# Up-projection, first pair of column blocks: the seventh product is subtracted earlier, and the spread of 1/rms stands one product later

## The chip, the cores and the metric

The kernel runs on one core of a Trainium2 chip. The core has a matrix engine (TensorE, PE in the profile, with PEld for its weight loads), a vector engine (VectorE, DVE), an engine for activations and copies (ScalarE, ACT), a further elementwise engine (GpSimd, POOL) and queues that issue DMA transfers (SyncE, SP, is the one used most). Each engine works through its own list of instructions in order, and waits for the others through semaphores. The metric is the time of one execution on the device, in microseconds (us); smaller is better.

## The reference

The program computes one layer of a decoder: normalisation, two attention branches with gates, a projection back, a residual sum, and then a gated feed-forward part with a short convolution, and a last normalisation. The change lies in the feed-forward part, whose heart is this:

```python
def rmsnorm(x, w):
    xf = x.astype(jnp.float32)
    y = xf * lax.rsqrt(jnp.mean(xf * xf, axis=-1, keepdims=True) + EPS)
    return (y * w.astype(jnp.float32)).astype(x.dtype)
...
def conv_ffn(xn, w_up, conv_w, conv_b, w_down):
    S = xn.shape[1]
    u = xn @ w_up
    upad = jnp.pad(u, ((0, 0), (CONV_WIDTH - 1, 0), (0, 0)))
    c = conv_b
    for j in range(CONV_WIDTH):
        c = c + upad[:, j:j + S] * conv_w[j]
    gate, val = jnp.split(c, 2, axis=-1)
    return (jax.nn.silu(gate) * val) @ w_down
...
        xn = rmsnorm(x, norm_ffn_w[l])
        x = x + conv_ffn(xn, w_up[l], conv_w[l], conv_b[l], w_down[l])
```

The sequence has 1024 positions, the model 1024 channels, and the up-projection 2 x 2816 columns. Everything is float32.

## The kernel before

All activations are kept transposed, channels on the 128 partitions and the 1024 positions along the free axis. A float32 product is made of three matmuls on parts: each operand is split into a high part (`wh`, `sh`, `B_..h`) and a low part (`wl`, `sl`, `B_..l`), and high by high, high by low and low by high are added up in PSUM, the accumulators that PE writes, which has eight banks. ACT makes the high part by a cast, DVE the low part by a subtraction; a *split* below is such a pair (lines 122 and 123).

The up-projection is the function `hidden`. Its 44 blocks of 128 columns are done in 22 pairs: block j of the gate half goes with block j + 22 of the value half. A pair is computed by a scheme of Strassen's kind, with seven products of half size in place of eight: P1, P2, P5, P7, P3, P6 and P4. Each is 12 matmuls of 128x512 (`product`, lines 877 to 885) into one bank. POOL makes the sums and differences of the weight blocks that the scheme needs (`sf`, lines 98 to 104), and these are then split (`sh`, `sl`). Afterwards the function `recombine` adds the products up into the four quarters of the result, `us`: a copy of P1 by ACT into `s1` (L426), and seven operations of DVE (L427 P2, L428 P6, L429 P7 into `u3`, L430 and L431 P5, L432 P3, L433 P4). A product's bank can be written again when the last of these has read it.

The normalisation is put off until after the product: the weights `norm_ffn_w` are multiplied into the operands, and the factor 1/rms of each position, `rstd`, is multiplied onto `us` when it is read for the convolution (L1038; on DVE for the first pair, on POOL for the others). 1/rms comes out of a sum over channels as a column of numbers per block of positions (`rs`, L197). To have it along the free axis on every partition, PE transposes it, broadcast, against the identity: this is the *spread* (`spread`, L203), in two halves of four transposes each, into the two banks of the pool `psC`. ACT copies each half into `rstd` (L966). For the first pair, one of these two banks held the sums over channels, `ssq`, and the other holds the product P4, since the six banks of the pool `psF` hold the other products. So the spread's second half can only be written when L433 has read P4.

Then the convolution follows in halves (`glu_halves`): two multiplications by `rstd`, an ACTIVATE of ACT with the centre tap and the bias (L1044), two operations of DVE with the other taps (L1046), Silu (L1048), the product with the value half (L1049) and a store to memory (`hd`, L1050).

The order of the instructions on each engine is set by a scheduling layer between this code and the program. It goes by its own estimate of when operands are ready, and by priorities; `issue_after(x)` makes what is issued within it stand behind instruction x on its engine. So a change at one place can move rows of other engines for some distance.

The first pair's order of work on PE is: the first three quarters of P1, P2, P5, P7, P3, then their last quarter and the sums over channels, then P6 and P4, then the first two products of the second pair (P1, P2), which need no waiting, then the spread, then the rest of the second pair.

Of the kernel before, what the change touches and what calls it, by code (L numbers as in the profile page):

```python
# [13 lines left out]
ALU = mybir.AluOpType  # L14
# [8 lines left out]
H2 = 512  # L23
# [20 lines left out]
class Trunk:  # L44
# [372 lines left out]
                        self.keep(m, u, (tp, "hi"))  # L417
        self.uw = self.w22 = None

    def recombine(self, ps, us, tp, o):  # L420

        nc = self.nc
        c11, c12, c21, c22 = (us[w][:, o + hf * H2:o + (hf + 1) * H2] for w in range(2) for hf in range(2))
        s1, u3 = (self.tl(tp, [P, H2], n, bufs=1) for n in ("s1", "u3"))
        tt = nc.vector.tensor_tensor
        nc.scalar.copy(s1, ps["P1"])  # L426
        tt(c11, ps["P2"], s1, ALU.add)  # L427
        tt(s1, ps["P6"], s1, ALU.add)  # L428
        tt(u3, ps["P7"], s1, ALU.add)  # L429
        tt(c22, ps["P5"], u3, ALU.add)  # L430
        tt(s1, ps["P5"], s1, ALU.add)  # L431
        tt(c12, ps["P3"], s1, ALU.add)  # L432
        return tt(c21, u3, ps["P4"], ALU.subtract)  # L433

    def keep(self, m, u, to):

# [432 lines left out]
    def product(self, ps, a, b, ks=range(4), first=True, last=True, skip=False, low_last=False):  # L869

        nc = self.nc
        ks = list(ks)
        ah, al = a
        if low_last:
            for n, k in enumerate(ks):
                for i, x in enumerate(self.B[b, k]):
                    nc.tensor.matmul(ps, ah[:, k, :], x, start=first and n == i == 0, stop=False, skip_group_check=skip)  # L877
            for n, k in enumerate(ks):
                nc.tensor.matmul(ps, al[:, k, :], self.B[b, k][0], start=False, stop=last and n == len(ks) - 1, skip_group_check=skip)
            return  # L880
        for n, k in enumerate(ks):
            bh, bl = self.B[b, k]
            nc.tensor.matmul(ps, ah[:, k, :], bh, start=first and n == 0, stop=False, skip_group_check=skip)  # L883
            nc.tensor.matmul(ps, ah[:, k, :], bl, start=False, stop=False, skip_group_check=skip)  # L884
            nc.tensor.matmul(ps, al[:, k, :], bh, start=False, stop=last and n == len(ks) - 1, skip_group_check=skip)  # L885

    def hidden(self, pair):
        nc, tc = self.nc, self.tc
        with ExitStack() as ctx:
# [6 lines left out]
            prods = (("P1", "A11", "B11"), ("P2", "A12", "B21"), ("P5", "S1", "T1"), ("P7", "S3", "T3"),  # L896
                     ("P3", "S4", "B22"), ("P6", "S2", "T2"), ("P4", "A22", "T4"))
# [3 lines left out]
            for j in range(NF):  # L901
                w, ps = ready.pop(j) if j else (w0, {})
                if j == 0:
# [10 lines left out]
                    tp = e(tc.tile_pool(name="tp", bufs=2, side="right", reuse_waits="tile"))  # L914
# [3 lines left out]
                    for n, (name, a, b) in enumerate(prods[:5]):  # L918
                        self.product(ps[name], w[a], b, (3,), first=False)
                        if n == 4:  # L920
                            self.col_sums(ssq, [self.rstd], NB, 0)
                            with tc.high_priority(400):
                                rs = self.rstd_cols(ssq, 8, D)
# [12 lines left out]
                us = [self.tl(tp, [P, T + 2], "us", bufs=3) for _ in range(2)]  # L936
                if j == NF - 1:
# [5 lines left out]
                    self.deep = True  # L943
                    with tc.high_priority(100):
                        self.ahead(2)
                c21 = self.recombine(ps, us, tp, 2)
                made = []
                if j < NF - 1:

                    self.after = c21 if j else None  # L950
                    w, ps = ready[j + 1] = self.next_w(), {}
                    self.after = None
                    if j:
                        made = [x[y] for x, y in ((w, ("made", "A22")), (self.wq[-1], ("made", "A11"))) if y in x]
                    if j == NF - 2:
                        raw = [self.tl(self.sfp[0], [P, T], "t42", bufs=1)] + [self.tl(self.sfp[0], [P, T], "sf") for _ in range(2)]
                        for k, r in enumerate(raw):
                            nc.sync.dma_start(r, self.hd[k])
                    for name, a, b in prods[:2 if j == 0 else 0]:
                        ps[name] = self.tl(psF, [P, H2], "t")  # L960
                        self.product(ps[name], w[a], b, low_last=name == "P1")
                if j == 0:
                    for hf in range(2):
                        sp = self.tl(self.psC, [P, H2], "c")
                        self.spread(sp, rs, hf * 4)
                        nc.scalar.copy(self.rstd[:, hf * H2:(hf + 1) * H2], sp)  # L966

                if j < NF - 2:
                    with ExitStack() as queue:
                        for i in made:  # L970
                            for x in i:
                                queue.enter_context(tc.issue_after(x.ins))
                        self.glu_halves(j, us)
                    continue
# [326 lines left out]
```

## Time and profile before

| what | value |
|---|---|
| time, median of 3 runs | 1354.51 us (1354.1 to 1355.41) |
| profiled execution, its time | 1354.84 us |
| profiled execution, its span from first to last instruction | 1353.1 us |
| mean granted clock of TensorE | 0.996 |
| up-projection in that span | about 690 to 1110 us |

In the profile's rows, an engine's name is followed by the source line, the operation, and the tiles that it writes and reads, output first. In a timeline the first two numbers are the start and the length in us; a bracket at the end gives the idle time of the engine just ahead of the row and what ended it. "xN" is the number of instructions in a row. In a list of waits, the three numbers are the sum in us, the number of waits and the longest. The names in these rows leave out the buffer numbers: `t` is a bank of the pool `psF`, `c` one of `psC` (or, from L1044 on, a buffer of the convolution), `s` is `s1` and `u` is `u3`.

### The profile page before, as it was taken

The numbers are of one execution on the slowest core, as the hardware profiler recorded it, in microseconds if no ns is written. First come the engines' busy times: TensorE is split into PE (matmuls) and PEld (weight loads), VectorE is DVE, ScalarE is ACT, GpSimd is POOL, SyncE is SP. The second block draws the span as 40 slices with busy tenths as digits, with TensorE's granted clock in tenths as the row PEclk, the third lists the DMA queues.
The fourth block names the chain that finished last, engine by engine and source line by source line (L and its number), as shares of the span: only waits on it lengthen the run. The fifth ranks groups of instructions, "written<-read, shape, count | busy, mean of one in ns | idle before, by whom it ended". The sixth has DMA issues, their size and how long they took to land.

```text
span 1353.1 us, 17298 instructions
## 1 busy us (share of the span) xinstructions
PE 1330.8 (98%) x6304; PEld 1105.7 (82%) x6304; DVE 1036.0 (77%) x1557; ACT 619.0 (46%) x1003; POOL 467.2 (35%) x349
## 2 busy tenths in 40 slices
PE   7999999999999999999998999999999999999997
PEld 6888888888887877878887888888888888888887
DVE  7846775288899875365679999999999977986454
ACT  8432232276667664334445344443444434333343
POOL 0436652010102125641454655555554510231011
PEclk9999999999999999999999999999999999999998
DMA  6423443966554236234422222222122238552342
GB/s 256 154 106 152 139 151 140 262 172 177 156 133 140 76 116 225 106 124 140 158 94 91 94 74 83 94 78 92 68 91 76 84 129 314 198 178 72 94 139 79
DMA packets 62468, 179.48 MB, mean 133 GB/s; under 512 B 6832, under 2 KB 15152, under 8 KB 62384
## 3 DMA queue, kind: packets, MB, share of 16 engines
q1 hardware_dynamic: 50928, 160.98, 36.5%
q10 hardware_dynamic: 11456, 17.41, 3.5%
q8 instruction: 49, 0.80, 0.2%
q14 instruction: 35, 0.29, 0.1%
HBM read 129.61 MB, written 48.76 MB: 132 GB/s over the span
## 4 chain that ended last, share of the span: by engine, by line
PE 87%; POOL 4%; DMA 3%; DVE 3%; issue 1%; ACT 1%; POOLq 0%; SPq 0%; ACTq 0%; DVEq 0%
PE t L883 13%; PE t L884 13%; PE t L885 13%; PE y L1086 3%; PE d L1086 3%; PE t L877 3%; PE sc L599 3%; PE g L180 3%; PE g L181 3%; PE g L182 3%; PE y L1113 2%; PE d L1113 2%; DMA gr<-gd 2%; PE sc L182 2%; PE sc L181 2%; PE sc L180 2%
## 5 line engine op out<-in xcount | busy, mean ns | idle before, releaser
L122 ACT CAST sh<-sf 128x1024 fp32r<-128x1024 f32 x62 | 65.1, 1051 | 111.4 <-PE t L884 91.8
L1046 DVE SCALAR_TENSOR_TENSOR c<-us,vecs,c 128x512 f32<-128x512 f32 x160 | 110.1, 748 | 4.3 <-ACT c L1044 4.3
L145 ACT CAST wh<-raw 128x1024 fp32r<-128x1024 f32 (+2 forms) x60 | 60.9, 1014 | 105.6 <-PE sc L181 30.5
L1038 POOL TENSOR_TENSOR us<-us,rstd 128x1024 f32<-128x1024 f32 x38 | 98.1, 2598 | 12.6 <-DVE us L433 5.3
L123 DVE TENSOR_TENSOR sl<-sf,sh 128x1024 fp32r<-128x1024 f32 x62 | 92.8, 1499 | 12.0 <-ACT sh L122 11.8
L147 DVE TENSOR_TENSOR wl<-raw,wh 128x1024 fp32r<-128x1024 f32 (+2 forms) x60 | 75.2, 1256 | 32.0 <-ACT wh L145 20.6
L1044 ACT ACTIVATE c<-us,vecs 128x512 f32<-128x512 f32 x80 | 61.2, 781 | 62.6 <-POOL us L1038 60.4
L123 DVE TENSOR_TENSOR wl<-raw,wh 128x1024 fp32r<-128x1024 f32 (+1 forms) x35 | 76.0, 2170 | 3.7 <-ACT wh L122 3.6
L98 POOL TENSOR_TENSOR sf<-rv 128x512 f32<-128x512 f32 x30 | 41.3, 1376 | 100.5 <-DVE sl L123 57.8
L180 PE MATMUL g<-xh,wh 128*128 128x512 f32 x176 | 70.7, 402 | 0.1
L182 PE MATMUL g<-xh,wl 128*128 128x512 f32 x176 | 70.4, 400 | 0.0
L181 PE MATMUL g<-xl,wh 128*128 128x512 f32 x176 | 70.3, 399 | 0.0
L197 POOL TENSOR_TENSOR rs<-ms,mhalf 128x8 f32<-128x8 f32 (+2 forms) x9 | 14.5, 1607 | 157.2 <-DVE ms L195 146.6
L103 POOL TENSOR_TENSOR sf<-raw,rv 128x512 f32<-128x512 f32 x30 | 40.7, 1357 | 67.3 <-DVE sl L123 67.3
L603 DVE CUSTOM_DVE_ANT_0 L<-sc,bias 128x128 f32<-128x128 f32 (+7 forms) x64 | 47.8, 752 | 17.0 <-PE sc L599 13.9
L604 ACT ACTIVATE L<-L,sm 128x128 f32<-128x128 f32 (+7 forms) x64 | 49.6, 779 | 20.0 <-DVE sm L603 17.3
L582 POOL MEMSET aT<- 128x128 f32 x32 | 6.2, 205 | 151.6 <-PE t L628 97.9
L757 POOL TENSOR_TENSOR gr<-gr,rstd 128x1024 f32<-128x1024 f32 x16 | 40.1, 2509 | 43.1 <-DMA gr<-gd 43.0
L1048 ACT ACTIVATE c<-c 128x512 f32<-128x512 f32 x40 | 24.0, 600 | 59.4 <-DVE c L1046 59.4
L599 PE MATMUL sc<-u,u 128*128 128x512 f32 (+2 forms) x192 | 49.7, 358 | 0.0
L182 PE MATMUL sc<-mh,wl 128*128 128x512 f32 x126 | 49.1, 390 | 0.2 <-DVE wl L147 0.2
L180 PE MATMUL sc<-mh,wh 128*128 128x512 f32 x126 | 49.0, 389 | 0.0
(515 smaller groups left out, 4330.8 us busy)
## 6 DMA issues: line engine op xcount, KB each, us to landing
u<-qd SPq DMA_DIRECT2D x72, 256.0 KB, 6.4
raw<-in_w_down SPq DMA_DIRECT2D x27, 512.0 KB, 3.7
raw<-in_w_in SPq DMA_DIRECT2D x25, 512.0 KB, 4.2
hr<-hd SPq DMA_DIRECT2D x50, 256.0 KB, 5.5
raw<-in_w_up SPq DMA_DIRECT2D x23, 512.0 KB, 3.4
hd<-c SPq DMA_DIRECT2D x22, 512.0 KB, 2.6
rv<-in_w_up SPq DMA_DIRECT2D x21, 512.0 KB, 3.4
gr<-gd SPq DMA_DIRECT2D x16, 512.0 KB, 3.5
```

The costliest lines, as they stand in the source:

```text
L123: j = nc.vector.tensor_tensor(lo, src, hi.bitcast(F32), ALU.subtract)
L147: self.lo = (eng or nc.vector).tensor_tensor(wl, raw, wh.bitcast(F32), ALU.subtract)
L180: nc.tensor.matmul(ps, wh[:, kc + o, :], ah, start=first and n == 0, stop=False)
L181: nc.tensor.matmul(ps, wh[:, kc + o, :], al, start=False, stop=False)
L182: nc.tensor.matmul(ps, wl[:, kc + o, :], ah, start=False, stop=last and n == len(kcs) - 1)
L599: nc.tensor.matmul(sc[:, lo + n0:lo + n1], qs, k[c][part][:, n0:n1], start=part == 0, stop=part == 1)
L883: nc.tensor.matmul(ps, ah[:, k, :], bh, start=first and n == 0, stop=False, skip_group_check=skip)
L884: nc.tensor.matmul(ps, ah[:, k, :], bl, start=False, stop=False, skip_group_check=skip)
L885: nc.tensor.matmul(ps, al[:, k, :], bh, start=False, stop=last and n == len(ks) - 1, skip_group_check=skip)
L1038: (nc.vector if j == 0 else nc.gpsimd).tensor_tensor(u[:, 2:], u[:, 2:], self.rstd, ALU.mult)
L1046: nc.vector.scalar_tensor_tensor(c, u[:, o + k:o + k + H2], col(m, k), c, ALU.mult, ALU.add)
L1086: nc.tensor.matmul(ps, v[:, n, :], x, start=n == i == 0, stop=n == len(js) - 1 and i == 2)
```

## The change

Three things are changed, all at the border between the first and the second pair:

1. `recombine` has a switch, `p4`, set for the first pair: the subtraction of P4 is written right behind `u3`, ahead of the two operations on P5. It gives no result then; the one that it gave was not used for the first pair.
2. The loop for the products that run ahead of the spread takes three in place of two, so the second pair's P5 is done ahead of the spread. The second half of the spread is ordered behind the last matmul of that product.
3. For the second pair, the copy of P1 into `s1` is ordered on ACT behind the spread's second copy.

`product` now gives back its last matmul, so that it can be used in the ordering.

```diff
-    def recombine(self, ps, us, tp, o):
+    def recombine(self, ps, us, tp, o, p4=False, after=None):
...
-        nc.scalar.copy(s1, ps["P1"])
+        with self.tc.issue_after(after.ins) if after is not None else nullcontext():
+            nc.scalar.copy(s1, ps["P1"])
         tt(c11, ps["P2"], s1, ALU.add)
         tt(s1, ps["P6"], s1, ALU.add)
         tt(u3, ps["P7"], s1, ALU.add)
+        if p4:
+            tt(c21, u3, ps["P4"], ALU.subtract)
         tt(c22, ps["P5"], u3, ALU.add)
         tt(s1, ps["P5"], s1, ALU.add)
         tt(c12, ps["P3"], s1, ALU.add)
-        return tt(c21, u3, ps["P4"], ALU.subtract)
+        return None if p4 else tt(c21, u3, ps["P4"], ALU.subtract)
...
-                c21 = self.recombine(ps, us, tp, 2)
+                c21 = self.recombine(ps, us, tp, 2, j == 0, made if j == 1 else None)
...
-                    self.after = c21 if j else None
+                    self.after = c21
...
-                    for name, a, b in prods[:2 if j == 0 else 0]:
+                    for name, a, b in prods[:3 if j == 0 else 0]:
                         ps[name] = self.tl(psF, [P, H2], "t")
-                        self.product(ps[name], w[a], b, low_last=name == "P1")
+                        last = self.product(ps[name], w[a], b, low_last=name == "P1")
                 if j == 0:
                     for hf in range(2):
                         sp = self.tl(self.psC, [P, H2], "c")
-                        self.spread(sp, rs, hf * 4)
-                        nc.scalar.copy(self.rstd[:, hf * H2:(hf + 1) * H2], sp)
+                        with tc.issue_after(last.ins) if hf else nullcontext():
+                            self.spread(sp, rs, hf * 4)
+                        made = nc.scalar.copy(self.rstd[:, hf * H2:(hf + 1) * H2], sp)
...
-                        for i in made:
+                        for i in made if j else ():
```

In the new file the lines of `recombine` behind its copy are one to three lines further down (L432 is P4 of the first pair, L433 and L434 P5, L435 P3, L436 P4 of the others), the copy into `rstd` is L971, the multiplication L1043 and the matmuls of `product` L886 to L888. The rows below show where the instructions stand, buffer numbers included.

On PE, at the end of the second pair's second product (`t_6528`), before:

```order
L885 MATMUL t_6528<-B_3h,wl_6474 128x512
L203 MATMUL c_6541<-ident,rs_6423 128x128 x4
L203 MATMUL c_6547<-ident,rs_6423 128x128 x4
L883 MATMUL t_6579<-T_0h,sh_6477 128x512
L884 MATMUL t_6579<-T_0l,sh_6477 128x512
```

and now, where the third product (`t_6541`, 12 matmuls, of which the last three are shown) has followed the second:

```order
L886 MATMUL t_6541<-T_3h,sh_6477 128x512
L887 MATMUL t_6541<-T_3l,sh_6477 128x512
L888 MATMUL t_6541<-T_3h,sl_6478 128x512
L203 MATMUL c_6554<-ident,rs_6423 128x128 x4
L203 MATMUL c_6560<-ident,rs_6423 128x128 x4
L886 MATMUL t_6592<-T_0h,sh_6477 128x512
```

The spread has moved behind a whole product; nothing else of PE's list has moved.

On DVE, in the first pair's recombination (`us_6451`, `us_6452`; `c_6438` is P4, `t_6344` P5, `t_6364` P3), before:

```order
L429 TENSOR_TENSOR u_1076_6454<-t_6354,s_1075_6453 128x512
L123 TENSOR_TENSOR sl_6504<-sf_6493,sh_6503 128x1024
L430 TENSOR_TENSOR us_6452<-t_6344,u_1076_6454 128x512
L431 TENSOR_TENSOR s_1075_6453<-t_6344,s_1075_6453 128x512
L433 TENSOR_TENSOR us_6452<-u_1076_6454,c_6438 128x512
L432 TENSOR_TENSOR us_6451<-t_6364,s_1075_6453 128x512
L123 TENSOR_TENSOR wl_6500<-raw_6489,wh_6499 128x1024
L427 TENSOR_TENSOR us_6644<-t_6528,s_1117_6646 128x512
L1038 TENSOR_TENSOR us_6451<-us_6451,rstd 128x1024
L1038 TENSOR_TENSOR us_6452<-us_6452,rstd 128x1024
```

and now:

```order
L123 TENSOR_TENSOR sl_6504<-sf_6493,sh_6503 128x1024
L432 TENSOR_TENSOR us_6452<-u_1076_6454,c_6438 128x512
L433 TENSOR_TENSOR us_6452<-t_6344,u_1076_6454 128x512
L434 TENSOR_TENSOR s_1075_6453<-t_6344,s_1075_6453 128x512
L123 TENSOR_TENSOR wl_6500<-raw_6489,wh_6499 128x1024
L435 TENSOR_TENSOR us_6451<-t_6364,s_1075_6453 128x512
L1043 TENSOR_TENSOR us_6451<-us_6451,rstd 128x1024
L1043 TENSOR_TENSOR us_6452<-us_6452,rstd 128x1024
L1051 SCALAR_TENSOR_TENSOR c_6571<-us_6451,vecs,c_6571 128x512
L428 TENSOR_TENSOR us_6644<-t_6528,s_1117_6646 128x512
L123 TENSOR_TENSOR sl_6508<-sf_6494,sh_6507 128x1024
```

The subtraction of P4 stands two rows earlier, a split has come ahead of the sum with P3, and the second pair's sum with P2 (`us_6644`) stands behind the multiplications by `rstd` and the convolution's first row. Behind this place DVE's rows stand in another order through the first four pairs, among them the split `sl_6671`, which has moved ahead of the end of the second pair's recombination.

On ACT, at the same place, before:

```order
L122 CAST wh_6499<-raw_6489 128x1024
L426 COPY s_1117_6646<-t_6515 128x512
L122 CAST wh_6666<-raw_6656 128x1024
L966 COPY rstd<-c_6541 128x512
L966 COPY rstd<-c_6547 128x512
```

and now:

```order
L122 CAST wh_6499<-raw_6489 128x1024
L122 CAST wh_6666<-raw_6656 128x1024
L971 COPY rstd<-c_6554 128x512
L971 COPY rstd<-c_6560 128x512
L427 COPY s_1117_6646<-t_6515 128x512
```

The copy of the second pair's P1 has gone behind the two copies of the spread. On POOL, the multiplications by `rstd` of the second pair (`us_6644`, `us_6645`) and the weight sums of the fifth (`sf_6815`), before:

```order
L1038 TENSOR_TENSOR us_6644<-us_6644,rstd 128x1024
L1038 TENSOR_TENSOR us_6645<-us_6645,rstd 128x1024
L98 TENSOR_TENSOR sf_6815<-rv_6813 128x512
L102 TENSOR_TENSOR sf_6815<-sf_6815,raw_6811 128x512
L1037 MEMSET us_6800 128x2
```

and now:

```order
L98 TENSOR_TENSOR sf_6815<-rv_6813 128x512
L102 TENSOR_TENSOR sf_6815<-sf_6815,raw_6811 128x512
L1043 TENSOR_TENSOR us_6644<-us_6644,rstd 128x1024
L1043 TENSOR_TENSOR us_6645<-us_6645,rstd 128x1024
L103 TENSOR_TENSOR sf_6816<-raw_6811,rv_6813 128x512
```

The multiplications stand behind two of the sums. On SP, the load of `rv_6813` stands ahead of the store of the first pair's result instead of behind it, and the load of the next raw weights ahead of the read of that store.

More of the change, by code (lines that the diff above doesn't have):

```diff
@@ L878, in product @@
             for n, k in enumerate(ks):
-                nc.tensor.matmul(ps, al[:, k, :], self.B[b, k][0], start=False, stop=last and n == len(ks) - 1, skip_group_check=skip)
-            return
+                i = nc.tensor.matmul(ps, al[:, k, :], self.B[b, k][0], start=False, stop=last and n == len(ks) - 1, skip_group_check=skip)
+            return i
         for n, k in enumerate(ks):
@@ L884, in product @@
             nc.tensor.matmul(ps, ah[:, k, :], bl, start=False, stop=False, skip_group_check=skip)
-            nc.tensor.matmul(ps, al[:, k, :], bh, start=False, stop=last and n == len(ks) - 1, skip_group_check=skip)
+            i = nc.tensor.matmul(ps, al[:, k, :], bh, start=False, stop=last and n == len(ks) - 1, skip_group_check=skip)
+        return i
     def hidden(self, pair):
```

## The prediction

> **What bounds the kernel now.** I read the page's busy times first, then TensorE's list of waits, then the timelines of the four engines around the one wait that the change touches, and at last the stretches of time by window.
>
> ```profile
> span 1353.1 us, 17298 instructions
> PE 1330.8 (98%) x6304; PEld 1105.7 (82%) x6304; DVE 1036.0 (77%) x1557; ACT 619.0 (46%) x1003; POOL 467.2 (35%) x349
> ```
>
> TensorE (PE) is busy for 98% of the span. What is left to win is its idle time, and the stretches in which it is busy at a lower clock. The waits of PE that are long enough to matter are few:
>
> ```profile
> PE t L306 <- ACT wh L145: 6.8, 1, 6.8
> PE c L203 <- DVE us L433: 4.0, 1, 4.0
> PE g L180 <- DVE gr L776: 1.5, 3, 0.8
> ```
>
> The first is the start of the kernel. The second is the one that this change is about: a transpose of the spread of 1/rms (L203) waits for the subtraction of P4 (L433). On PE it looks like this (start, length, engine, instruction):
>
> ```profile
> 709.52 0.60 PE L203 MATMUL c<-ident,rs 128*128 128x128 f32 x4
> 714.10 0.86 PE L203 MATMUL c<-ident,rs 128*128 128x128 f32 x4 [3.99 <-DVE us L433]
> 714.62 0.77 PE L883 MATMUL t<-T_0h,sh 128*128 128x512 f32 x1
> ...
> 718.72 0.39 PE L885 MATMUL t<-T_3h,sl 128*128 128x512 f32 x1
> 718.95 0.40 PE L883 MATMUL t<-T_0h,sh 128*128 128x512 f32 x1
> ```
>
> The first half of the spread runs at 709.52, the second half stands for 3.99 us, and then the second pair's product P5 (714.62 to 718.95) takes 4.33 us for its 12 matmuls. At the normal spacing, 718.95 - 718.72 = 0.23 us (0.227 unrounded over a product), 12 matmuls are 2.72 us. The windows say why (columns: length, busy time of PE, PEld, DVE, ACT, POOL, then the granted clock):
>
> ```profile
> 690.00:709.00 19.00, 19.00 (x93) 16.02 (x92) 17.33 (x16) 7.77 (x9) 14.08 (x10) 1.00 0.11 33
> 714.40:717.80 3.40, 3.40 (x12) 2.72 (x11) 2.54 (x4) 2.50 (x4) 2.48 (x2) 0.50 0.26 55
> 480.00:560.00 80.00, 78.59 (x352) 62.88 (x351) 46.25 (x67) 41.66 (x60) 37.10 (x17) 1.00 0.44 162
> ```
>
> The granted clock is 1.00 ahead of the wait and 0.50 for the 3.4 us behind it. The waits of up to 0.8 us (PE g L180, all in 480 to 560) left it at 1.00. So the stall costs 3.99 + (4.33 - 2.72) = 5.6 us.
>
> **Why PE stands: the other engines.** First DVE, then ACT, POOL:
>
> ```profile
> 706.62 0.68 DVE L428 TENSOR_TENSOR s<-t,s 128x512 f32<-128x512 f32 x1
> 708.69 0.68 DVE L429 TENSOR_TENSOR u<-t,s 128x512 f32<-128x512 f32 x1
> 711.03 1.23 DVE L123 TENSOR_TENSOR sl<-sf,sh 128x1024 fp32r<-128x1024 f32 x1 [1.66 <-ACT sh L122]
> 712.17 0.68 DVE L430 TENSOR_TENSOR us<-t,u 128x512 f32<-128x512 f32 x1
> 712.77 0.68 DVE L431 TENSOR_TENSOR s<-t,s 128x512 f32<-128x512 f32 x1
> 713.37 0.68 DVE L433 TENSOR_TENSOR us<-u,c 128x512 f32<-128x512 f32 x1
> 713.96 0.69 DVE L432 TENSOR_TENSOR us<-t,s 128x512 f32<-128x512 f32 x1
> 714.56 1.25 DVE L123 TENSOR_TENSOR wl<-raw,wh 128x1024 fp32r<-128x1024 f32 x1
> 715.74 0.68 DVE L427 TENSOR_TENSOR us<-t,s 128x512 f32<-128x512 f32 x1
> 717.28 2.36 DVE L1038 TENSOR_TENSOR us<-us,rstd 128x1024 f32<-128x1024 f32 x2 [0.86 <-ACT rstd L966]
> ```
> ```profile
> 709.95 1.05 ACT L122 CAST sh<-sf 128x1024 fp32r<-128x1024 f32 x1 [3.98 <-POOL sf L102]
> 714.74 0.59 ACT L426 COPY s<-t 128x512 f32<-128x512 f32 x1 [2.80 <-DVE us L432]
> 716.17 1.07 ACT L966 COPY rstd<-c 128x512 f32<-128x512 f32 x2
> ```
>
> DVE starts a row every 0.60 us here. The subtraction of P4 comes third behind a split (sl, 711.03) that itself waits for ACT, which waits for POOL. None of those three rows is touched by the change, so 711.03 stays.
>
> **The change, part by part.**
>
> The subtraction moved up: it takes the place of L430, at 712.17, and its bank is free at 712.17 + 0.68 = 712.85, with the wake-up of the row above (713.37 + 0.68 = 714.05, PE at 714.10) 712.90 for PE. That alone is 1.20 us earlier. No instruction is added: c22 and the sum behind it come 0.60 later each. P5's old bank is free at 714.05 instead of 713.45. P7 of the second pair reuses it, and comes at about 716.1 (below), so this costs nothing. The added ordering of the second half behind the product's last matmul costs nothing, since PE runs in that order anyway.
>
> The spread one product later: PE has the product P5 of the second pair (12 x 0.227 = 2.72 us) to do first, 709.52 to 712.24. It needs its operands (the split that ended ahead of the sum at 706.62) and a bank: the built program gives it the bank of the first pair's P6, whose last reader is that sum at 706.62, ended 707.30. So it does not wait. The first half then takes 712.24 to 712.68 (709.52 0.60 is four transposes that start 0.11 apart), the second could start at 712.68 and gets its bank at 712.90: a wait of 0.2 us in place of 3.99. P6 of the second pair starts at 712.90 + 0.44 = 713.34 instead of 718.95. This is the term of the sum: -5.61 us.
>
> The clock: 1.6 of the 5.61 us rests on the 0.2 us wait leaving the clock alone. The nearest rows are the three waits of up to 0.8 us that did. The rows leave open what a wait between 0.8 and 3.99 us does; a new wait of 2 to 3 us could cost 1.6 more. [...]
>
> The copies ahead of the next recombination: ACT's two copies of 1/rms follow the halves of the spread, so they end near 714.1 instead of 717.24. The copy of P1 (714.74), which they now precede, still waits for L432, which moves behind a split (1.25 less its overlap, 1.2) and to about 715.2; so the copy comes at 715.9, 1.1 us later. The multiplications by 1/rms then follow L432 at once, at about 715.8 instead of 717.28, and the 0.86 us wait of DVE is gone. P2's sum (715.74) moves behind them, to some 718.7. P2's bank is next written by the third pair's P1, which PE reaches at 713.34 plus four products, 724.2. So nothing on PE waits there.
>
> **What is late next.** PE is now 5.6 us ahead of its old time, but DVE is not, for its rows are nearly back to back. So the slack of PE against DVE shrinks by 5.6 us, for the rest of this stage. Where it was tightest, as end of the releasing row and start of the matmul on that bank:
>
> ```profile
> 729.94 0.68 DVE L431 TENSOR_TENSOR s<-t,s 128x512 f32<-128x512 f32 x1
> 763.68 0.68 DVE L428 TENSOR_TENSOR s<-t,s 128x512 f32<-128x512 f32 x1
> 1112.24 0.68 DVE L432 TENSOR_TENSOR us<-t,s 128x512 f32<-128x512 f32 x1
> ```
> ```profile
> 738.01 0.39 PE L883 MATMUL t<-T_0h,sh 128*128 128x512 f32 x1
> 770.65 0.39 PE L883 MATMUL t<-B_0h,wh 128*128 128x512 f32 x1
> 1114.73 0.61 PE L1113 MATMUL d<-sh,wh 128*128 128x512 f32 x2
> ```
>
> 738.01 - 730.62 = 7.4 us in the third pair; 770.65 - 764.36 = 6.3 us in the fifth; 1114.73 - 1112.92 = 1.8 us where the stage ends. In the third pair 1.8 us remain. In the fifth 0.7 us remain if DVE stays at its old time. Does it? It wins the 0.86 us, and a split of 3.02 us moves ahead to a place where POOL stands idle. Against that, POOL's multiplications of the second pair (731.90) come behind two POOL rows that need a load:
>
> ```profile
> 731.90 4.94 POOL L1038 TENSOR_TENSOR us<-us,rstd 128x1024 f32<-128x1024 f32 x2 [3.87 <-DVE us L432]
> 756.52 1.29 POOL L98 TENSOR_TENSOR sf<-rv 128x512 f32<-128x512 f32 x1 [1.68 <-DMA rv<-in_w_up]
> ```
> ```profile
> 734.91 3.02 DVE L123 TENSOR_TENSOR sl<-sf,sh 128x1024 fp32r<-128x1024 f32 x1
> 768.13 1.22 DVE L123 TENSOR_TENSOR sl<-sf,sh 128x1024 fp32r<-128x1024 f32 x1
> ```
> ```profile
> 753.01 0.33 SPq L95 DMA_DIRECT2D rv<-in_w_up  x1
> ```
>
> A load issued at 753.01 reached POOL at 756.52, 3.5 us. The load in question is issued behind a split that stands twelve rows behind the multiplications, which end at 718.1; at 0.6 to 1.2 us a row that is near 726.6, so POOL starts its first row near 730.1, its multiplications near 732.8, 0.9 us later than 731.90, and the second pair's convolution on DVE is later by as much, while the rows moved ahead save about as much. SP issues this load ahead of the store of the first pair instead of behind it; the store's reader is the last pair, so that costs nothing. I take DVE as unmoved at the fifth pair (bounds: 0.9 us earlier, 1.5 later): PE waits 0 to 0.8 us there, taken 0.1.
>
> From there DVE catches up:
>
> ```profile
> 750.00:769.00 19.00, 19.00 (x85) 15.75 (x84) 18.42 (x22) 8.22 (x11) 10.85 (x9) 1.00 0.25 84
> 882.37 0.69 DVE L433 TENSOR_TENSOR us<-u,t 128x512 f32<-128x512 f32 x1 [0.37 <-PE t L885]
> 1102.69 0.69 DVE L428 TENSOR_TENSOR s<-t,s 128x512 f32<-128x512 f32 x1 [1.56 <-PE t L885]
> ```
>
> It is busy 18.42 of 19.00 us, so it can win some 0.3 to 0.6 us per pair, in 17 pairs 5 to 10 us; before, it had started to wait for PE at 882.37, eight pairs in. By the last pair at most some 2 us are left, and there DVE had 1.56 us of waiting for PE to spend. I take a wait of 0.2 us at 1114.73 (bounds 0 and 1.2). Behind it all engines move together.
>
> **The sum.** -5.61 + 0.1 + 0.2 = -5.3 us. The profiled execution took 1354.84 us (span 1353.1 and 1.74 around it), so 1349.5; the median of the runs, 1354.51, lies 0.33 lower: 1349.2.
>
> **The rivals.**
> - DVE becomes the bound in the first pairs. For it: it is nearly full, its rows are reordered for four pairs, and the same split takes 3.02 us beside POOL's multiplications and 1.22 alone (734.91, 768.13), so each such split that falls beside them costs 1.8 us. If DVE falls L late at the fifth pair, PE waits L - 0.7. With one split L = 0.9 + 1.8 = 2.7, the gain is 5.3 - 2.0 = 3.3: 1351.2. Against it: the waits that go, and that the split at 734.91 leaves POOL's neighbourhood. [...]
> - The clock still halves after the shorter wait: 1349.2 + 1.6 = 1350.8. For it: the 0.50 row; against it: the waits of 0.8 us at 1.00.
> - The change doesn't do what it says: the early product waits for its bank, or the split ahead of the subtraction comes later. If P5 waited for the L431 row (713.45, now 714.05), PE would idle 4.6 us, run the product at half clock and the spread behind it: P6 near 719.4, 1355.0. Against it: the bank is that of P6, free at 707.30.
> - Slower: the same lag of DVE, deeper. From L = 4.7 PE's wait is 4.0 us and halves the clock as the old one did, 1.6 us more, so that the gain is gone; from L = 7.1 it is slower by 0.2%, and at L = 8 the time is 1349.2 + 7.3 + 1.6 = 1358.1. Against it: DVE gets no instruction more, and it would take four splits beside POOL at 1.8 us each.
>
> **How the numbers follow.** Forecast 0.66; DVE as the bound 0.17 (0.02 of it past 1351.8); half clock 0.05; no effect 0.06; slower 0.06. A measurement of this kernel tells changes from about 0.2% (2.7 us) apart, 1351.8 and 1357.2. Faster 0.66 + 0.15 + 0.05 = 0.86, same 0.02 + 0.06 = 0.08, slower 0.06. The range: below, the 5.61 with DVE's 0.5 us of luck, 1348.4; above, DVE as the bound with L = 3.5, 1352.0.
>
> **What would show it.** In the changed profile: the 4.0 us entry of PE for the spread's bank shrinks to some 0.2; no 0.50 in the clock near 714; P6 of the second pair starts at 713.3. Wrong if PE shows new waits for DVE's sums (L428 now L429, L431 now L434) between 730 and 780, or at the stage's end.

## The result, and the profile after

The changed kernel takes 1349.17 us (median of 6 runs, 1345.76 to 1350.06), the kernel before 1354.96 us (median of 6 runs, 1353.7 to 1357.16) on the same chip. The ratio is 0.9953, with a 95% interval from 0.994 to 0.9966: 0.5% faster. The prediction was 1349.2 us. One execution in all the runs told here, of the kernel with the early subtraction alone, was slow (1910.09 us at a granted clock of 0.654): the ratios are of fast runs alone, and that kernel's median, 1352.12 us with it, is 1351.82 us without.

The page of the changed kernel, and the head of TensorE's list of waits (sum, number, longest, in us):

```profile
span 1347.3 us, 17300 instructions
PE 1328.9 (99%) x6304; PEld 1104.6 (82%) x6304; DVE 1036.0 (77%) x1557; ACT 616.1 (46%) x1003; POOL 470.6 (35%) x349
```
```profile
PE t L306 <- ACT wh L145: 7.0, 1, 7.0
PE g L180 <- DVE gr L779: 1.5, 2, 0.9
```

The span is 5.8 us shorter. The 4.0 us entry for the spread's bank is gone, and no other has come in its place. The timeline of PE at the spread (start, length), and the windows (length, busy time of PE, PEld, DVE, ACT and POOL, then the granted clock):

```profile
709.49 0.39 PE L888 MATMUL t<-B_3h,wl 128*128 128x512 f32 x1
709.72 0.39 PE L886 MATMUL t<-T_0h,sh 128*128 128x512 f32 x1
...
712.44 1.33 PE L203 MATMUL c<-ident,rs 128*128 128x128 f32 x8
713.53 0.48 PE L886 MATMUL t<-T_0h,sh 128*128 128x512 f32 x1
...
716.37 0.39 PE L886 MATMUL t<-T_0h,sh 128*128 128x512 f32 x1
```
```profile
714.00:717.80 3.80, 3.80 (x19) 3.10 (x18) 3.70 (x4) 0.98 (x2) 3.14 (x2) 1.00 0.20 30
```

Product P5 of the second pair follows P2 without a gap, the eight transposes of the spread run in one row, P6 follows at 713.53 and P7 at 716.37, all at a clock of 1.00. (From the second pair on the order is P1, P2, P5, P6, P7, P3, P4, with P6 ahead of P7; the last pair alone differs.) A *stretch* below is the time from the last matmul of the second pair's P2 to the first of its P7: two products and the spread, the same work in every kernel here but the one with four products. Here it is 716.37 - 709.49 = 6.88 us; in the kernel before, by these two rows, it is 12.40 us:

```profile
709.29 0.39 PE L885 MATMUL t<-B_3h,wl 128*128 128x512 f32 x1
...
721.69 0.39 PE L883 MATMUL t<-T_0h,sh 128*128 128x512 f32 x1
```

So 5.52 of the 5.8 us are won at this place. PE's rows, matched one by one with those of before, keep this lead unchanged to the end of the stage. The other 0.3 us come near 1180, and every other kernel tried here has 0.1 to 0.3 us of it too, the slower ones included: that belongs to the profiled execution of before, not to the change. Between 500 and 600, far ahead of the change, the profiled executions drift apart by up to 3 us. Hence the stretches tell the parts apart better than the times.

The other engines at the same place, DVE and then ACT:

```profile
711.24 1.23 DVE L123 TENSOR_TENSOR sl<-sf,sh 128x1024 fp32r<-128x1024 f32 x1 [1.67 <-ACT sh L122]
712.38 0.68 DVE L432 TENSOR_TENSOR us<-u,c 128x512 f32<-128x512 f32 x1
...
714.18 1.88 DVE L123 TENSOR_TENSOR wl<-raw,wh 128x1024 fp32r<-128x1024 f32 x1
715.98 0.68 DVE L435 TENSOR_TENSOR us<-t,s 128x512 f32<-128x512 f32 x1
716.76 2.67 DVE L1043 TENSOR_TENSOR us<-us,rstd 128x1024 f32<-128x1024 f32 x2
```
```profile
713.08 1.32 ACT L971 COPY rstd<-c 128x512 f32<-128x512 f32 x2
716.69 0.59 ACT L427 COPY s<-t 128x512 f32<-128x512 f32 x1 [2.30 <-DVE us L435]
```

The subtraction of P4 (L432) ends at 713.06, when the first half of the spread has just run; the second half starts 0.06 us behind that end. The copies into `rstd` are done by 714.40, so the multiplications (L1043) need not wait for them, although the copy of P1 waits until 716.69.

### The profile page after: what moved, and what is told of

It is laid out like the page before. It is cut to its first block, busy times and chain, and to the rows that moved or that the text cites. A ratio compares the mean times of both kernels' runs of the same rounds, so it can differ in the third digit from the quotient of the medians.

```text
span 1347.3 us, 17300 instructions
## 1 busy us (share of the span) xinstructions
PE 1328.9 (99%) x6304; PEld 1104.6 (82%) x6304; DVE 1036.0 (77%) x1557; ACT 616.1 (46%) x1003; POOL 470.6 (35%) x349
## 4 chain that ended last, share of the span: by engine, by line
PE 88%; POOL 4%; DVE 3%; DMA 3%; ACT 1%; issue 1%; POOLq 0%; SPq 0%; ACTq 0%; DVEq 0%
PE t L886 13%; PE t L887 13%; PE t L888 13%; PE y L1091 3%; PE d L1091 3%; PE t L880 3%; PE g L180 3%; PE sc L602 3%; PE g L181 3%; PE g L182 3%; PE y L1118 2%; PE d L1118 2%; DMA gr<-gd 2%; PE sc L182 2%; PE sc L181 2%; PE sc L180 2%
## 5 line engine op out<-in xcount | busy, mean ns | idle before, releaser
L1043 POOL TENSOR_TENSOR us<-us,rstd 128x1024 f32<-128x1024 f32 x38 | 99.6, 2641 | 4.5 <-DVE us L435 2.4
L123 DVE TENSOR_TENSOR sl<-sf,sh 128x1024 fp32r<-128x1024 f32 x62 | 87.5, 1413 | 11.5 <-ACT sh L122 11.5
L123 DVE TENSOR_TENSOR wl<-rv,wh 128x512 fp32r<-128x512 f32 x30 | 49.3, 1642 | 3.5 <-ACT wh L122 3.5
```

The costliest lines, as they stand in the source:

```text
L123: j = nc.vector.tensor_tensor(lo, src, hi.bitcast(F32), ALU.subtract)
L1043: (nc.vector if j == 0 else nc.gpsimd).tensor_tensor(u[:, 2:], u[:, 2:], self.rstd, ALU.mult)
```

## The experiments

Each edit is shown against the kernel before or against the changed kernel, as said. The kernels were timed beside the kernel before in three groups: the first four told here (before: 1354.53 us), the four with additions of SBUF tiles (1354.27 us), and the remaining three (1354.70 us).

### The product ahead, alone

Against the kernel before, one number:

```diff
-                    for name, a, b in prods[:2 if j == 0 else 0]:
+                    for name, a, b in prods[:3 if j == 0 else 0]:
```

> The third product ahead of the spread, without the early subtraction of P4 and without the order of the copies. My theory: the second half of the spread can start at 712.7 and its bank is free at 714.1 (the subtraction stays the third row behind the split at 711.0), so TensorE waits 1.4 us. If a wait of that length leaves the clock at 1.00, the gain is 5.6 - 1.2 = 4.4 us against before, 0.9 us less than the whole change. Rival (the clock halves behind any wait over some 0.8 us): a stretch at 0.50 behind the wait, and a gain of about 2.8 us. Second rival (the order of the copies carries part of the gain): DVE's multiplications by 1/rms come late and TensorE shows new waits between 730 and 780.

PE's wait, and the window behind it:

```profile
712.99 0.65 PE L203 MATMUL c<-ident,rs 128*128 128x128 f32 x4 [1.27 <-DVE us L433]
```
```profile
713.00:717.00 4.00, 4.00 (x20) 3.37 (x21) 3.14 (x4) 2.51 (x4) 2.79 (x2) 1.00 0.29 70
```

The stretch is 8.07 us, 4.33 less than before; no new waits behind it. The time is 1348.79 us against 1354.53 (ratio 0.9958, 0.9944 to 0.9971). The theory holds: this part carries 4.3 of the 5.5 us, and the wait of 1.27 us left the clock alone.

### The early subtraction, alone

Against the kernel before: the switch `p4` of `recombine`, and nothing else of the change.

```diff
+        if p4:
+            tt(c21, u3, ps["P4"], ALU.subtract)
...
-                c21 = self.recombine(ps, us, tp, 2)
+                c21 = self.recombine(ps, us, tp, 2, j == 0)
```

> The early subtraction of P4 alone; the spread stays behind the second product. My theory: the bank is free 1.2 us earlier, so TensorE waits 2.8 us in place of 4.0. If the halved clock needs a whole window of idleness of some 3.4 us, the clock stays at 1.00 and the gain is 1.2 + 1.6 = 2.8 us. Rival (the clock halves behind a wait well under that): 0.50 is seen behind it and the gain is 1.2 us only. Second rival (the early subtraction is what matters, and the product ahead is not): the gain is near the whole change's 5.3 us.

```profile
711.09 1.12 PE L203 MATMUL c<-ident,rs 128*128 128x128 f32 x4 [2.78 <-DVE us L431]
```
```profile
707.70:711.12 3.42, 0.64 (x6) 0.39 (x4) 1.91 (x3) 1.99 (x2) 3.42 (x3) 1.00 0.48 153
711.12:714.53 3.41, 3.41 (x10) 2.87 (x11) 3.41 (x4) 0.00 (x0) 3.29 (x4) 0.50 0.00 0
```

The wait is 1.2 us shorter, and the clock still halves, from 711.12 to 714.53, so that P5 takes 4.07 us (711.86 to 715.93) in place of 2.72. The stretch is 11.17 us, 1.23 less than before; the time 1352.12 us (ratio 0.9982, 0.9972 to 0.9991). The first rival holds: 2.78 us of idleness were enough to halve the clock, so this part alone is worth its 1.2 us and no more.

### The bank alone

Against the kernel before: the spread's second half goes into a bank of `psF`, whose next free one is that of P7, and P4 is not in its way. Nothing is moved.

```diff
-                        sp = self.tl(self.psC, [P, H2], "c")
+                        sp = self.tl(psF, [P, H2], "t") if hf else self.tl(self.psC, [P, H2], "c")
```

> The order of before, but the second half of the spread goes into a bank of the six for the products instead of P4's, so it does not wait for the subtraction of P4. My theory (the whole gain is the wait for that bank and the clock behind it): no wait for the spread at 709.96, no 0.50, and a gain of 5.6 us, less what the products behind it wait for the bank that has been taken, 0 to 0.8 us. Rival (the gain needs the product's 2.7 us as cover, since DVE is late anyway): the wait moves to the next product's bank, and TensorE waits 2 us or more there.

```profile
708.78 0.60 PE L203 MATMUL c<-ident,rs 128*128 128x128 f32 x4
709.22 0.60 PE L203 MATMUL t<-ident,rs 128*128 128x128 f32 x4
...
712.76 0.50 PE L883 MATMUL t<-T_0h,sh 128*128 128x512 f32 x1 [0.18 <-DVE s L431]
```

Both halves run back to back, P6 waits 0.18 us for the bank of P5, and the stretch is 7.08 us, 5.32 less than before. Of this lead 0.4 us are lost where the stage ends (below, with the four products). The time is 1349.57 us (ratio 0.9963, 0.9951 to 0.9976). So nearly the whole gain (5.3 of 5.5 us) is the wait for P4's bank and the clock behind it; to move the spread is one way to avoid it, to write elsewhere is another.

### Without the order of the copies

Against the changed kernel: the copy of P1 is not ordered behind the copies into `rstd`.

```diff
-                c21 = self.recombine(ps, us, tp, 2, j == 0, made if j == 1 else None)
+                c21 = self.recombine(ps, us, tp, 2, j == 0, None)
```

> The whole change without the third part, the order of P1's copy behind the copies of 1/rms. My theory: this part moves work of ACT and DVE that has slack to spare, so the time is that of the whole change within 0.5 us, 5.3 us under before, with a wait of at most 0.2 us at the spread. Rival (the copies of 1/rms held up by the copy of P1 delay the multiplications and with them DVE): TensorE shows new waits for DVE's sums in the next pairs and 1 to 2 us of the gain are lost.

DVE, ACT, and PE's list of waits:

```profile
717.32 0.69 DVE L428 TENSOR_TENSOR us<-t,s 128x512 f32<-128x512 f32 x1 [0.71 <-ACT s L427]
719.24 2.36 DVE L1043 TENSOR_TENSOR us<-us,rstd 128x1024 f32<-128x1024 f32 x2 [1.23 <-ACT rstd L971]
```
```profile
718.14 1.07 ACT L971 COPY rstd<-c 128x512 f32<-128x512 f32 x2
```
```profile
PE t L886 <- DVE s L434: 0.8, 1, 0.8
...
PE t L886 <- DVE s L429: 0.4, 1, 0.4
```

The stretch is the changed kernel's, 6.89 us. But the copies into `rstd` come 5 us later (718.14 against 713.08), behind the copy of P1, which waits for L435; DVE waits twice, 1.94 us, and is 2.2 us late at the convolution's first row (721.52 against 719.36, where the spread starts 0.04 us apart). In the third pair PE then waits 0.77 us, in the sixth 0.42, and by 800 the lead of 5.5 us over the kernel before is down to 3.5. The time is 1350.54 us (ratio 0.9974, 0.9965 to 0.9983). My theory fell here, the rival holds: the order of the copies keeps 2 us of the gain. It is needed because of the early subtraction, which sends L435 behind a split: with the product alone, where that sum stays ahead of the split, PE had no such waits.

### A longer wait, twice not as meant

To see which wait halves the clock, three additions (and in a second kernel four) were put into the changed kernel ahead of the early subtraction:

```diff
+            for o in (c12, c22, c12):
+                tt(o, u3, s1, ALU.add)
             tt(c21, u3, ps["P4"], ALU.subtract)
```

> The whole change, with three additions of 128x512 that do nothing useful put ahead of the early subtraction of P4, each some 0.6 us: TensorE's wait at the spread grows from 0.06 to 1.9 us. The product-only kernel's 1.27 us wait left the clock at 1.00 and the subtraction-only kernel's 2.78 us wait halved it. If the bound lies above 1.9: clock 1.00, and the second pair's P6 comes 1.8 us later than with the change. If below: 0.50 for some 3.4 us behind the wait and 1.4 us more, 3.2 us in all. DVE and TensorE are late together, so no new waits behind.

> The same with four additions: a wait of 2.5 us. Theory (any wait that fills most of a window of 3.4 us halves the clock, as 2.78 us did): 0.50 behind it, and TensorE 2.4 + 1.4 = 3.8 us later than with the change. Rival (the bound lies between 2.5 and 2.78): 1.00 and 2.4 us later.

The waits were 5.10 and 5.70 us. With three, the additions as DVE's group (count, busy us, mean ns), the wait, three windows, and one of POOL's rows at that time:

```profile
L433 DVE TENSOR_TENSOR us<-u,s 128x512 f32<-128x512 f32 x3 | 5.1, 1750 | 0.0
```
```profile
717.68 1.12 PE L203 MATMUL c<-ident,rs 128*128 128x128 f32 x4 [5.10 <-DVE us L434]
```
```profile
711.48:714.90 3.42, 1.10 (x7) 0.68 (x6) 3.42 (x3) 1.72 (x3) 3.30 (x4) 1.00 0.01 2
714.90:718.31 3.41, 0.63 (x3) 0.63 (x4) 3.41 (x5) 0.00 (x0) 1.57 (x1) 0.50 0.00 0
718.31:721.72 3.41, 3.41 (x11) 2.74 (x10) 3.31 (x4) 1.17 (x2) 0.00 (x0) 0.50 0.20 31
```
```profile
713.22 1.59 POOL L98 TENSOR_TENSOR sf<-rv 128x512 f32<-128x512 f32 x1
```

An addition took 1.75 us on average in place of 0.6: both its inputs lie in SBUF, and POOL was working on SBUF beside it (three that read PSUM took 1.88 us in all, below). Four of them took 5.71 us in all: the last, which ran when POOL's rows there were over (at 714.79), added only some 0.6. With four, the first half of the spread, and the windows ahead of the idle one and behind it:

```profile
710.29 0.60 PE L203 MATMUL c<-ident,rs 128*128 128x128 f32 x4
```
```profile
709.14:712.55 3.41, 1.75 (x10) 1.24 (x8) 3.41 (x3) 2.37 (x3) 3.37 (x4) 1.00 0.17 67
715.96:719.38 3.42, 2.79 (x9) 2.40 (x10) 3.42 (x5) 0.59 (x1) 0.00 (x0) 0.50 0.02 5
```

The stretches are 13.78 and 13.80 us, 1.4 more than before, and the times 1355.64 and 1355.41 us (ratios 1.0012, 1.0001 to 1.0023, and 1.0019, 1.0009 to 1.0029). The question was not answered at 1.9 us, but the drop of the clock is seen inside a wait: with three additions at 714.90, 2.3 us after PE's last row had ended (711.98 + 0.60), and with four at 715.96, 5.1 us after it (710.29 + 0.60). With three the half clock lasts to 721.72, 6.83 us, twice the 3.41 us of the early subtraction alone; with four it lasts 3.41 us.

The third kernel has three additions that read P5's bank in PSUM in place of the tile `s1`:

```diff
+            for o in (c12, c22, c12):
+                tt(o, ps["P5"], u3, ALU.add)
             tt(c21, u3, ps["P4"], ALU.subtract)
```

> The whole change, with three useless additions again ahead of the early subtraction of P4, but each reads P5's bank of PSUM and u3 instead of two tiles of SBUF. Theory (the additions of two SBUF tiles took 1.75 us each because POOL's sums of weights ran beside them): these take 0.6 us each, and TensorE waits 1.9 us in place of 0.06. Rival (whatever stands there is slow): 5.1 us again. On the clock: if a window 3.4 us long halves it only when most of it is idle, a wait of 1.9 us (56% of a window at most) lies between the 49% that left it and the 68% that halved it, so either 1.00 and 1.8 us later than with the change, or 0.50 and 3.2 us later.

```profile
L433 DVE TENSOR_TENSOR us<-t,u 128x512 f32<-128x512 f32 x3 | 1.9, 682 | 0.0
```
```profile
713.46 0.65 PE L203 MATMUL c<-ident,rs 128*128 128x128 f32 x4 [1.88 <-DVE us L434]
```
```profile
710.09:713.50 3.41, 1.53 (x10) 1.08 (x8) 3.41 (x6) 2.11 (x3) 3.37 (x3) 1.00 0.08 34
713.50:716.91 3.41, 3.41 (x17) 2.90 (x18) 3.31 (x5) 0.91 (x2) 1.30 (x2) 1.00 0.02 5
```

At the same place, each takes 0.68 us (three of them 1.88), the wait is 1.88 us, and the clock stays at 1.00 in the profiled execution. The stretch is 8.69 us, 1.81 more than with the change; the time 1351.83 us (ratio 0.9974, 0.9963 to 0.9985). Only one execution of each kernel has a profile: of this kernel's ten, five have a mean granted clock of 0.996 in place of the profiled one's 0.998, and a stretch of 3.41 us at half clock is 0.0013 of it. So it may have fallen in some of the others; no trace here shows that.

### DVE made late

In the changed kernel, additions in the second pair's recombination, ahead of its sums with P5: two in one kernel, seven in the other.

```diff
+        for _ in range(idle):
+            tt(c22, u3, s1, ALU.add)
         tt(c22, ps["P5"], u3, ALU.add)
```

> The whole change, with two useless additions (1.2 us of DVE) in the second pair's recombination, ahead of its sums with P5. In the profile of the changed kernel the third pair's P6 has 1.5 us of slack against the DVE row that frees its bank. The two additions and one row that the scheduling layer moves ahead make that row 1.9 us later. Theory (slack swallows what fits): TensorE waits some 0.3 us there, and little more later: the time is the changed kernel's within 0.6 us. Rival (DVE has no slack at all): the full 1.2 to 1.9 us.

> The same with seven useless additions (4.2 us of DVE). Theory: the row that frees the bank of the third pair's P6 is some 5.5 us later (4.2 for the additions and two rows that move ahead), less 1.5 of slack: TensorE waits 4.0 us, the clock halves behind it for 1.4 to 1.6 us more, and the whole gain of 5.5 us is gone, the time is that of before within 1 us. Rival (DVE catches up in its own waits of 3.4 and 1.2 us in the second pair before TensorE needs it): TensorE loses 1 us or less.

The waits of PE in the third pair, with two additions and then with seven, and the clock of the latter:

```profile
730.71 0.50 PE L888 MATMUL t<-T_0h,sh 128*128 128x512 f32 x1 [0.17 <-DVE s L436]
```
```profile
731.94 0.50 PE L888 MATMUL t<-T_0h,sh 128*128 128x512 f32 x1 [1.17 <-DVE us L438]
...
737.63 0.47 PE L888 MATMUL t<-T_0h,sh 128*128 128x512 f32 x1 [2.67 <-DVE s L436]
```
```profile
733.14:736.55 3.41, 1.82 (x8) 1.16 (x7) 3.31 (x5) 1.05 (x1) 0.00 (x0) 1.00 0.35 101
736.55:739.96 3.41, 2.33 (x10) 1.97 (x11) 3.38 (x4) 0.59 (x1) 2.99 (x2) 1.00 0.51 207
739.96:743.37 3.41, 3.41 (x16) 2.83 (x16) 1.30 (x3) 1.43 (x2) 3.41 (x3) 1.00 0.00 0
```

With two, PE loses 0.5 us in all and nothing later; the time is 1347.36 us (ratio 0.9953, 0.9935 to 0.9971). With seven, it loses 1.5 and 2.9 us; the time is 1352.54 us (ratio 0.9992, 0.998 to 1.0003). Both follow the theory in kind: the slack swallows what fits, the rest is paid, and with some 5 us of lag nearly all of the gain is gone. In size the second missed: the waits add up to 3.84 us, but lie in two pieces, one for the subtraction of P4 (L438), which the scheduling layer put between the additions, and one for the sum with P5 (L436). Neither halved the clock, though one is 2.67 us long (the last section has why).

### One product more

Against the changed kernel, `prods[:4 if j == 0 else 0]`.

> The whole change, with four products ahead of the spread in place of three. Theory (with three the wait is already down to 0.06 us): nothing is left to win at the spread; the copies of 1/rms come 2.7 us later, near 717.1, some 0.4 us later than the multiplications started, and the slack of 1.5 us in the third pair takes that: the time is the changed kernel's within 0.3 us. Rival (later copies delay DVE and POOL): new waits of TensorE in the third pair, as without the order of the copies, 0.5 to 2 us lost.

```profile
PE d L1118 <- DVE us L435: 2.2, 1, 2.2
```

At the spread PE is 5.8 us ahead of before, 0.3 more than with three products, and DVE has no trouble (its multiplications wait 0.21 us). But where the stage ends, the first product of the down-projection waits 2.2 us for the last pair's sum with P3, and the lead falls to 3.3 us. The time is 1350.44 us (ratio 0.9968, 0.9953 to 0.9982). Neither theory had this. It is a matter of banks: the six banks of `psF` are handed out in turn as they come free, a bank more taken at the first pair shifts that through all 22 pairs, and the down-projection's products use fixed banks. In the built program P3 of the last pair has the bank of the down-projection's third product before and with the change, that of its second with the bank alone, and that of its first here. These products start 2.04 us apart.

### The bank and the order of the copies

Against the kernel before: the edit of the bank alone, and the third part of the change.

```diff
-                        sp = self.tl(self.psC, [P, H2], "c")
+                        sp = self.tl(psF, [P, H2], "t") if hf else self.tl(self.psC, [P, H2], "c")
...
+        with self.tc.issue_after(after.ins) if after is not None else nullcontext():
+            nc.scalar.copy(s1, ps["P1"])
```

> The spread's second half in a bank of the products' pool, at its old place, and the copy of P1 ordered behind the copies of 1/rms; no product moved and no early subtraction. Theory: no wait for P4's bank; the second pair's P6 waits some 0.2 to 0.3 us for P5's bank, as with the bank alone, and DVE no longer waits 0.8 us for the copies, so the 0.4 us that the bank alone lost at the end of the stage is not lost: a gain of 5.3 to 5.6 us, the same as the changed kernel's. Rival (DVE's earlier rows collide with POOL's): 0.5 to 2 us less.

```profile
710.58 0.50 PE L884 MATMUL t<-T_0h,sh 128*128 128x512 f32 x1 [0.20 <-DVE s L432]
...
1105.09 0.73 PE L1114 MATMUL y<-sl,wh 128*128 128x512 f32 x2 [0.49 <-DVE us L433]
```

The stretch is 7.09 us (5.31 less than before). At the end of the stage 0.8 us are lost, not 0: the second product of the down-projection waits for P3's bank. The time is 1347.92 us (ratio 0.9957, 0.9942 to 0.9972). By its interval this is no better than the changed kernel, and neither is any other kernel of this study.

## Why the prediction was right

**The time.** The gain was forecast at 5.3 us and came out at 5.8, with 4.6 to 8.1 inside the ratio's interval. That the time agrees to 0.1 us is luck: the kernel before took 1354.96 us beside the changed one, where the prediction had started from 1354.51, and the two differences cancel.

**The stall and its clock (term -5.61 us).** Confirmed: the stretch shrank by 5.52 us. P6 was to start at 713.34; it starts at 713.53, in an execution that is 0.20 us late at P2 already. The subtraction was to start at 712.17, and 712.38 less the same 0.20 is that. The wait of 0.2 us left at the spread was there in effect (0.08 us in the profile's own count): the eight transposes took 1.33 us, where with four products ahead, and no wait, they took 1.04. The single parts also have the predicted sizes: 4.33 us for the product with the subtraction left third (expected 4.4), 1.23 for the subtraction (1.20).

**The clock.** The prediction left open what a wait between 0.8 and 3.99 us does. In the profiled executions, 1.27 and 1.88 us left the clock at 1.00, 2.78 us halved it and cost 1.35 us more than itself (P5 took 4.07 us in place of 2.72), and 2.67 us did not halve it, because a border of the clock's windows cut that wait in two (last section). What the prediction needed, that the wait of 0.2 us is harmless, held in any case. Its estimate that a new wait of 2 to 3 us could cost 1.6 us more came out at 1.35 for the 2.78 us, and at nothing for the 2.67.

**The copies.** Here the working was incomplete, though the sum came out. It had the order right (the copies first, the multiplications at once behind the sum with P3), and it had that sum behind a split, at 715.2; it came at 715.98, 715.78 without the 0.20, because the split took 1.88 us and not 1.25. It wrote that nothing on PE waits there, and gave the third part no price of its own. That is true of the change as a whole, but it is the third part that makes it true: without it 2 us of the gain were lost.

**What is late next (terms +0.1 and +0.2).** Both were zero. The slack that is left, as end of DVE's row and start of PE's, in the third pair, in the fifth and at the end of the stage of the changed kernel:

```profile
730.49 0.68 DVE L434 TENSOR_TENSOR s<-t,s 128x512 f32<-128x512 f32 x1
...
762.37 0.68 DVE L429 TENSOR_TENSOR s<-t,s 128x512 f32<-128x512 f32 x1
...
1107.32 0.68 DVE L435 TENSOR_TENSOR us<-t,s 128x512 f32<-128x512 f32 x1
```
```profile
732.69 0.39 PE L886 MATMUL t<-T_0h,sh 128*128 128x512 f32 x1
...
765.33 0.39 PE L886 MATMUL t<-B_0h,wh 128*128 128x512 f32 x1
...
1109.41 0.62 PE L1118 MATMUL d<-sh,wh 128*128 128x512 f32 x2
```

That is 1.5 us in the third pair (predicted 1.8) and 1.4 us at the end (predicted 1.8 - 5.6 + what DVE catches up, taken as a wait of 0.2): there DVE's row ended 4.9 us earlier than before (1108.00, 1112.92), so DVE had caught up with nearly all of PE's lead. So the sum, -5.3 us, was 0.2 us short at the place.

In the fifth pair PE was to have 0.7 us left and to wait 0.1; it had 2.3 us, 1.3 of them by a reordering that the prediction did not have. It took the row that frees the bank, the fourth pair's sum with P6, as unmoved, with a bound of 0.9 us earlier. That row started at 762.37 (L429) in place of 763.68 (L428), 1.3 us earlier, because the scheduling layer had put it ahead of the convolution's last row and of the product behind that. DVE as a whole was unmoved, as taken: the next sum, with P7, began at 765.4 before and now. One pair on, where the sum with P6 stands at its old time (782.39, before 782.45), PE had 1.3 us left.

One estimate on this path was off without harm: POOL's multiplications of the second pair came at 735.21 and not at 732.8, behind a sum that took 2.17 us, and DVE waited 3.36 us for them by way of ACT.

**The rivals.** DVE as the bound did not come about, but it is a true danger and not a distant one: with the order of the copies left out DVE is 2.2 us late and PE pays 2 us, with seven additions 4.4 us. Where the deeper lag was to cost the whole gain (a single wait of 4.0 us with half a clock behind it), seven additions left 1.1 us of it in the profiled execution, since the wait came in two pieces; by the times, that kernel can't be told from the one before. The subtraction's split did not move, and the bank of P5's product was free, as taken. The 1.22 us of a split alone stands in the profile of before at 764.28; the row cited for it, at 768.13, took as long, but had POOL's row at 768.29 (2.91 us) beside it.

## What to carry to other kernels

The stall of the matrix engine had two prices here, its length (3.99 us) and the half clock behind it (1.6 us more), and with a wait of 1.27 us the second was gone. So it pays to look whether such a stall can be shortened, even where it can't be removed; the longest wait that left the clock alone within one of its windows was 1.88 us here. When a row is pulled ahead to free a buffer early, look at what it pushes back on its engine, and at which queue then waits for that: here the pushed row held a copy on another engine, and behind it the copies that everyone needed. Count buffer rotations too: one more buffer taken in a ring moves the one that is late to another user, even hundreds of microseconds further on.

## What was not expected of the hardware

- *The clock changed on a fixed grid, and part of a window was enough.* In all 13 profiled executions, every change of the granted clock in the trace lies a whole number of steps of 3.4133 us behind the first. In the kernel before, it rises at 11.25, falls at 714.40, rises at 717.81 and falls at 1345.86: 206, 207 and 391 steps behind the first; in the changed kernel it rises at 12.18 and falls at 1339.96, 389 steps behind. So the borders of the windows are known in every execution, also where the clock does not change, and the windows shown above with 3.41 or 3.42 us go from border to border. In the window ahead of the four falls at the spread, PE was idle, by its rows, for 91% (before, 710.99 to 714.40), 81% (early subtraction), 68% (three additions) and 100% (four). The clock stayed where it was idle for 37% (the product alone, 710.05 to 713.46), 49% (four additions, up to 712.55), 55% (the wait of 1.88 us), and 47% and 32% (seven additions, where the border at 736.55 cuts the wait of 2.67 us). So by these executions the bound lies between 55% and 68% of a window, 1.9 to 2.3 us, and what a wait somewhat longer than that cost depended on where it met the grid: 2.78 us (early subtraction) halved the clock, 2.67 us (seven additions) did not. At the end of the kernel the clock falls too, behind windows that by their rows are idle for 34% to 76%; many of these rows are matmuls of one column, whose listed ends are modelled, and without them it is 62% to 83%, which fits.
- *A wait cost some 0.3 us more than it lists.* With two and seven additions, waits of 0.17, 1.17 and 2.67 us put PE back by 0.48, 1.46 and 2.95 us. The row of a matmul lasts 0.39 us where the next starts 0.23 after it, and the second matmul behind a wait starts 0.31 to 0.34 us after the first.
- *The same addition cost 0.6 or 1.75 us at the same place,* by whether one of its inputs lay in PSUM (three took 1.88 us) or both in SBUF (three took 5.09 us), while POOL worked on SBUF. POOL's two rows there took 1.59 us each in the kernel with both inputs in SBUF, 1.27 and 1.30 us in the other. The times of the two kernels show this much; what in the hardware makes it so, they do not show.
